# Moving the modulation's vectors one place later in a transformer kernel, and queueing VectorE's part of them behind the MLP step they belong to

## The chip, the cores and the metric

The kernel runs on one core of one Trainium2 chip. The metric is the device time of one execution in microseconds. Work is spread over TensorE (matmuls, with its weight loads beside them), VectorE, ScalarE and GpSimd; all loads of this kernel are issued from SyncE's queue.

## The reference

One token block of 256 tokens with 1024 features goes through two blocks of layers. The first has a mixer (a gated MLP over tokens beside a linear recurrence) and a mixture of 32 experts. The second has two layers, the first with a sparse attention of three branches, the second with a differential attention, and an MLP behind each. In the second block a condition vector modulates every layer:

```
cond = silu(c)                                    # 1024 values
for i in range(2):
    mod = cond @ w_ada[i] + b_ada[i]              # 6 vectors of 1024
    sh1, sc1, g1, sh2, sc2, g2 = split(mod, 6)
    h = rms_norm(x, ln_mix_g[i]) * (1 + sc1) + sh1
    x = x + g1 * mixer_i(h)
    h = rms_norm(x, ln_mlp_g[i]) * (1 + sc2) + sh2
    x = x + g2 * (square(relu(h @ w_mlp_in[i])) @ w_mlp_out[i])
```

The kernel numbers these vectors 0 to 11: vector 6 i + 0 and 1 are shift and scale in front of the mixer of layer i, 2 its gate, 3 and 4 shift and scale in front of the MLP, 5 the MLP's gate. Each is the product of 1024 condition values with a matrix of 1024 x 1024, 4 MB of weights that are read once.

## The kernel before, in words

**Order of work.** The program is written with a framework that plans the order of instructions on each engine and each queue: instructions are written down in program order, and a planner that simulates the engines with its own costs picks, at each point, an instruction whose inputs it takes to be ready, earlier ones first. An instruction may thus run well ahead of the place where it is written. `tc.issue_after(ins)` keeps the instructions that are written inside it behind `ins` on the engine of `ins`. On the chip each engine then works through its planned list.

**Weights.** Every weight tile of 1 MB is loaded by `load` (line 131) from SyncE's queue into one of eight buffers of a ring; a load waits until a buffer has been read out. Matmul operands are split into a high and a low part (`whi` by ScalarE at line 151, `wlo` by VectorE at line 152, in three buffers each), and three products are summed.

**The modulation's vectors.** `ada_at` holds which vector is next and how far it is. There are two ways to make one:

- On TensorE, in two halves. `ada_half` runs `ada_tiles`: two loads of 1 MB and 16 matmuls, each of which uses a strip of 32 columns of the array (line 187; two records each in the trace), then one VectorE copy or addition into `adaacc` (lines 211, 214).
- On VectorE, in four quarters. `ada_vector` loads 1 MB and multiplies it by the condition, one operation for each of its two rows of 1024 (lines 256 and 258), summed in `adasum`. Behind the fourth quarter TensorE sums over the partitions with four strip matmuls against ones, and ScalarE copies the result.

`ada_close` ends a vector: four small products with `pick` (line 225), and a VectorE addition of the bias that writes `mods[v]` (line 228). It is called where the next piece of a vector begins, or where `ada_until` or the second half of an out-projection (`out_late`) asks for it.

Where they stand before: five halves in the first block, seven in the sparse attention (`work(j)` for j = 3 to 9; this makes vectors 2 to 5 complete), vectors 6 to 10 as quarters in the first MLP (`vectors` is 11), and vector 11 in four fills of one tile at the end of that MLP and in the norm behind it (`Stats.fill`). The second MLP is called with `vectors` 12, at which nothing is left.

**The attention.** `attention` runs over 16 units (head pair i, token half m), three stages deep: `pair_probs` of unit j (scores, maximum, exponential), `pair_out` of unit j - 1 (reciprocal, gate, scaling of the probabilities `p`, transposes, product with the values), `pair_tail` of unit j - 2, and `work(j)` in between, which from j = 10 on adds the first half of the out-projection (`oearly`). The second half (`olate`) follows behind the last unit, and feeds the MLP's input through `feed`.

**The MLP.** `mlp` has nine steps. Step j makes 512 hidden features (`hp`, line 448, 96 products), scales, squares and splits them (`relu`, `hid`, lines 1739 to 1745), and then adds the previous step's hidden features to the result (`rows`, line 491, 96 products). From j = 1 on, each step may call `ada_vector` twice behind the hidden features and once between the two halves of `rows`.

Of the kernel before, what the change touches and what calls it, by code (L numbers as in the profile page):

```python
# [13 lines left out]
F32 = mybir.dt.float32  # L14
# [7 lines left out]
ALU = mybir.AluOpType  # L22
# [22 lines left out]
def block_kernel(ctx: ExitStack, tc: tile.TileContext, A: dict, out: bass.AP):  # L45

    nc = tc.nc
# [8 lines left out]
    def mm(shape=(P, 512), name="mm"):  # L56
        return mm_pool.tile(list(shape), F32, tag="mm", name=name)
# [4 lines left out]
    def sc(shape=(P, 512), name="sc"):  # L62
        return scratch.tile(list(shape), F32, tag="sc", name=name)
# [61 lines left out]
    def load(src, c, pool=None, tag="w", cut=1):  # L125

        t = (pool or next(source[0])).tile([P, 2048], F32, tag=tag, name="w")
        v = t[:, : src.shape[1] * c].rearrange("p (k c) -> p k c", c=c)
        n = src.shape[1] // cut
        for i in range(cut):  # L130
            loaded.append(nc.sync.dma_start(v[:, i * n : (i + 1) * n, :], src[:, i * n : (i + 1) * n, :]))
        load_small(SMALL)
        return v
# [40 lines left out]
    mods = [const.tile([P, KD], F32, name=f"mod{v}") for v in range(12)]  # L174
# [9 lines left out]
    def strips(ps, lhsT, w, start, stop):  # L184

        for j in range(4):
            nc.tensor.matmul(ps[32 * j : 32 * j + 32, :], lhsT, w[:, j * T : (j + 1) * T], start=start, stop=stop)  # L187
# [30 lines left out]
    def ada_close():  # L218

        if not ada_open:  # L220
            return
        v = ada_open.pop()
        sp = mm(name="adasum")
        for c in range(2):
            nc.tensor.matmul(
                sp[:, 4 * c : 4 * c + 4], ada_acc[:, c * P : (c + 1) * P], pick, start=True, stop=True
            )
        nc.vector.tensor_tensor(
            mods[v].rearrange("p (j c) -> p c j", c=2),
            sp[:, 0:8].rearrange("p (c j) -> p c j", c=2),  # L230
            col("ada", v * KD, KD).rearrange("p (j c) -> p c j", c=2),
            op=ALU.add,
        )

    def ada_half(behind=(None,)):
        for _ in ada_tiles(behind):
            pass
# [4 lines left out]
            ada_at[2] -= 2.0  # L242
            ada_half()

    def ada_vector(acc):

        ada_close()
        v, q, _ = ada_at
        lay, i = divmod(v, 6)
        w = load(  # L250
            A["w_ada_2"][lay, 2 * q * P : 2 * (q + 1) * P, i * D : (i + 1) * D].rearrange("(k p) c -> p k c", p=P), D
        )
        for kk in range(2):
            c = cond[:, 2 * q + kk : 2 * q + kk + 1]
            if q + kk == 0:
                nc.vector.tensor_scalar(acc, w[:, kk, :], c, None, op0=ALU.mult)
            else:
                nc.vector.scalar_tensor_tensor(acc, w[:, kk, :], c, acc, op0=ALU.mult, op1=ALU.add)
        ada_at[1] = q + 1
        if q == 3:  # L260
            ps = mm(name="adaps")[:, :T]
            strips(ps, ones[:, 0:32], acc, True, True)
            nc.scalar.copy(ada_acc, ps)
            ada_at[:2] = [v + 1, 0]
            ada_open.append(v)
# [247 lines left out]
    def add_pair(pr, bank, gate=None):  # L513

        v = res[:, 2 * pr : 2 * pr + 2, :]
        if gate is None:
            added[0] = nc.vector.tensor_tensor(v, bank, v, op=ALU.add)
        else:
            for j in range(2):
                k = 2 * pr + j  # L520
                nc.vector.scalar_tensor_tensor(
                    res[:, k, :], bank[:, j, :], gate[:, k : k + 1], res[:, k, :], op0=ALU.mult, op1=ALU.add
                )
        return v

    def closing(banks, gate=None, st=None, each=None, feed=None):

        def after(pr):  # L530
            v = add_pair(pr, banks[pr], gate)
            last = pr == KD // 2 - 1
            if feed is not None:
                feed(pr)
                st.square(pr, v)
                if pr >= 2:
                    st.count(pr - 2)
                return
            if st is not None:
                if last and st.w is not None:  # L540
                    held["first"]["dve"] = added[0]
                st.square(pr, v)
            if st is not None:
                for p in range(pr - 2, pr + 1 if last else pr - 1):
                    if last and p == pr and st.w is None:
                        st.fill()
                    if p >= 0:
                        st.count(p)
            if each is not None:
                for p in range(pr - 1, pr + 1 if last else pr):  # L550
                    if p >= 0:
                        each(p)

        return after
# [96 lines left out]
    with tc.tile_pool(name="pa", bufs=1, reuse_waits="tile") as pa:  # L651

        def pt(name, shape=(P, 4, T), tag=None, dt=F32):
            return pa.tile(list(shape), dt, name=name, tag=tag or name)
# [145 lines left out]
        q = pt("q")  # L800
# [200 lines left out]
        r = rstd_of(gss, P, "v")  # L1001
        for m in range(2):
            for h in range(4):
# [5 lines left out]
                    op0=ALU.mult,  # L1009
                    op1=ALU.mult,  # L1010
# [21 lines left out]
        for g in range(4):  # L1032
# [5 lines left out]
                op0=ALU.add,  # L1038
                op1=ALU.mult,
# [37 lines left out]
    with (  # L1077
# [6 lines left out]
        def bt(name, shape, dt=F32, tag=None):  # L1084
# [30 lines left out]
            op=ALU.add,  # L1115
# [23 lines left out]
        for i in range(2):  # L1139
# [5 lines left out]
                op=ALU.is_equal,  # L1145
# [478 lines left out]
        st = Stats(finsq)  # L1624
# [8 lines left out]
    def ct(name, shape, dt=F32, tag=None, **kw):  # L1633
        return pc.tile(list(shape), dt, name=name, tag=tag or name, **kw)

    def n8(name, dt=F32):
        return pc.tile([P, 2048], dt, tag="n8", name=name, bufs=2)
# [80 lines left out]
    def mlp(lay, close, st, vectors):  # L1718

        ada_sum = ct("adasum", (P, D), tag="klo")  # L1720
        if ada_at[1]:
            ada_half()
        w_i, w_o = A["w_mlp_in_2"][lay], A["w_mlp_out_2"][lay]
        pend = None
        for j in range(9):
            rate[0] = 0.0
            if j < 8:
                hp = [(mm if j else acc)((P, TX), name="hp") for _ in range(4)]
                for n, _ in enumerate(proj_X_steps(w_i, j * 512, hp)):
                    if j == 0 and n == 3:  # L1730
                        st.count(2)
                        st.count(3)
                        rb = st.scale()
                both = n8("hid", F32R).rearrange("p (a k t) -> p a k t", a=2, k=4)
                for i in range(2):
                    r = sc((P, 2, T), name="relu")
                    b = pw.tile([P, 4], F32, tag="nm", name="hb")
                    for c in range(2):
                        nc.vector.tensor_copy(b[:, c : c + 1], hp[2 * i + c][:, T : T + 1])
                        nc.vector.tensor_tensor(r[:, c, :], hp[2 * i + c][:, 0:T], rb, op=ALU.mult)  # L1740
                        nc.scalar.activation(r[:, c, :], r[:, c, :], AF.Relu, bias=b[:, c : c + 1])
                    hi = both[:, 0, 2 * i : 2 * i + 2, :]
                    nc.scalar.activation(hi, r, AF.Square)
                    nc.scalar.activation(r, r, AF.Square)
                    nc.vector.tensor_tensor(both[:, 1, 2 * i : 2 * i + 2, :], r, hi.bitcast(F32), op=ALU.subtract)
                for _ in range(2):
                    if j and ada_at[0] < vectors:
                        ada_vector(ada_sum)
            if j == 0:
                banks = [acc((P, 2, T), name="mlp") for _ in range(4)]  # L1750
            if pend is not None:
                jj, bb = pend
                if jj == 7:
                    ada_close()
                    ada_until(6 * lay + 6)
                for c in (0, 2):
                    if c == 2 and ada_at[0] < vectors:
                        ada_vector(ada_sum)
                    after = close(banks) if jj == 7 and c == 2 else None
                    rows(w_o, jj * 4 + c, banks, (bb[:, 0], bb[:, 1]), c, jj == 0 and c == 0, after)  # L1760
            pend = (j, both)
# [16 lines left out]
    both = mm((P, 2, T), name="rbps")  # L1778
# [378 lines left out]
    def work(j):  # L2157
        chains.tick(3)
        if 1 <= j < 5:
            steps(second, 3)  # L2160
        elif j >= 10:
            steps(first, 1)
        if 3 <= j < 10:
            ada_half()

    attention([(i, m) for i in range(8) for m in (1, 0)], pair_probs, pair_out, pair_tail, work)
# [3 lines left out]
    st_x = Stats(plain=True)  # L2170
# [12 lines left out]
    nc.vector.tensor_tensor(nlam, ls[:, 1:2], ls[:, 0:1], op=ALU.subtract)  # L2183
    nc.vector.tensor_scalar(nlam, nlam, -lam_init, None, op0=ALU.add)
    st = Stats()
    mlp(0, lambda banks: closing(banks, mods[5], st), st_x, 11)


    modulated(st, 1, 0, col("lnx", 8, 8))
# [109 lines left out]
    st = Stats(plain=True)  # L2299
# [46 lines left out]
```

## Time and profile before

| | |
|---|---|
| Median of three runs | 1307.72 us (1306.44 to 1311.22) |
| The profiled execution | 1306.74 us, of which the span of the profile is 1305.0 us |
| Granted clock of TensorE, mean | 0.995 |
| TensorE busy | 97% of the span |
| VectorE, ScalarE busy | 50%, 39% |
| Read from HBM | 371.41 MB, 285 GB/s over the span |

Times in the rows are microseconds from the start of the span. A row of the timeline gives start, busy time, engine, line, operation, output and inputs, the number of instructions that were merged, and in brackets how long the engine stood idle before it and what ended that. Engines are PE (TensorE), DVE (VectorE), ACT (ScalarE), POOL (GpSimd), SPq (SyncE's queue of loads). Matmuls overlap in a pipeline, so the sum of their durations is more than the time they take.

### The profile page before, as it was taken

What the parts mean: (1) busy time and instruction counts of PE and PEld (TensorE: products, weight loads), DVE (VectorE), ACT (ScalarE), POOL (GpSimd) and SP (SyncE); (2) the same over time, 40 slices, a digit from 0 to 9 for tenths busy, and PEclk for the clock granted to TensorE, in tenths of its full rate; (3) what the DMA queues carried; (4) which work ended last, traced back from release to release, by engine and by line L of the source; (5) the groups of instructions that cost most, each with busy time, mean ns of one, the idle gap of its engine ahead of it and who ended that gap; (6) DMA issues with size and microseconds to landing.
All of it is one profiled execution on the core that took longest, in us unless ns stands there. A gap on an engine that the chain in (4) does not pass through costs nothing.

```text
span 1305.0 us, 22821 instructions
## 1 busy us (share of the span) xinstructions
PE 1263.6 (97%) x9471; PEld 1001.2 (77%) x9471; DVE 652.6 (50%) x1268; ACT 512.6 (39%) x918; POOL 68.4 (5%) x92
## 2 busy tenths in 40 slices
PE   8999899999999999999999999999999999999998
PEld 7779565665555555556886679999997779999998
DVE  6765310220101111105786777688766777655554
ACT  7743210111101111104555646545444565654644
POOL 1010000000000000000410000000001221000000
PEclk9999999999999999998999999999999999999999
DMA  7997799999999999998545846699677432555510
GB/s 252 369 411 302 305 421 420 420 421 421 422 420 420 421 421 421 420 413 296 186 156 193 323 140 212 206 353 338 244 256 259 161 130 76 180 173 187 194 66 33
DMA packets 99157, 373.98 MB, mean 287 GB/s; under 512 B 10649, under 2 KB 14442, under 8 KB 74730
## 3 DMA queue, kind: packets, MB, share of 16 engines
q1 hardware_dynamic: 99050, 372.49, 74.8%
q8 instruction: 76, 1.25, 0.4%
q14 instruction: 31, 0.25, 0.1%
HBM read 371.41 MB, written 1.05 MB: 285 GB/s over the span
## 4 chain that ended last, share of the span: by engine, by line
PE 74%; issue 11%; DVE 2%; ACT 1%; POOL 0%; DVEq 0%; ACTq 0%; POOLq 0%
PE hp L448 14%; PE mlp L491 14%; PE gups L1413 12%; PE dps L1443 6%; PE dps L469 5%; PE sums L1461 3%; PE gps L1367 2%; PE oearly L584 2%; PE qp L469 2%; PE olate L491 2%; PE adaps L187 1%; PE kv L469 1%; PE opair L2098 1%; PE kcv L469 1%; PE ptps L2089 1%
## 5 line engine op out<-in xcount | busy, mean ns | idle before, releaser
L152 DVE TENSOR_TENSOR wlo<-w,whi 128x1024 fp32r<-128x1024 f32 (+1 forms) x222 | 269.7, 1217 | 158.0 <-ACT whi L151 155.9
L151 ACT CAST whi<-w 128x1024 fp32r<-128x1024 f32 (+1 forms) x222 | 230.4, 1042 | 249.3 <-PE hp L448 105.6
L1413 PE MATMUL gups<-w,xg 128*64 128x256 f32 x2048 | 233.7, 381 | 3.8 <-PEq L1271 2.8
L1413 PEld LDWEIGHTS gups<-w,xg 128*64 128x64 f32 x2048 | 145.1, 137 | 90.0 <-issue 19.4
L491 PE MATMUL mlp<-hid,whi 128*128 128x256 f32 x1024 | 184.0, 282 | 0.0
L491 PEld LDWEIGHTS mlp<-hid,whi 128*128 128x128 f32 x1024 | 157.2, 188 | 0.4 <-issue 0.4
L491 PE MATMUL mlp<-hid,wlo 128*128 128x256 f32 x512 | 144.8, 283 | 0.0
L448 PE MATMUL hp<-hT_lo,whi 128*128 128x258 f32 x512 | 144.0, 282 | 0.0
L448 PE MATMUL hp<-hT_hi,whi 128*128 128x258 f32 x512 | 143.7, 283 | 0.0
L448 PE MATMUL hp<-hT_hi,wlo 128*128 128x258 f32 x512 | 142.5, 282 | 0.0
L1425 DVE TENSOR_TENSOR h<-h,gups 128x256 f32<-128x256 f32 x32 | 13.5, 421 | 235.7 <-ACT h L1424 235.7
L1443 PE MATMUL dps<-w,hT 128*64 128x512 f32 x496 | 112.7, 596 | 5.0 <-ACT hT L1433 5.0
L491 PEld LDWEIGHTS mlp<-hid,wlo 128*128 128x128 f32 x512 | 96.4, 188 | 1.6 <-issue 1.6
L448 PEld LDWEIGHTS hp<-hT_lo,whi 128*128 128x128 f32 x512 | 96.7, 189 | 0.0
L448 PEld LDWEIGHTS hp<-hT_hi,whi 128*128 128x128 f32 x512 | 96.1, 188 | 0.0
L448 PEld LDWEIGHTS hp<-hT_hi,wlo 128*128 128x128 f32 x512 | 95.9, 189 | 0.0
L1424 ACT ACTIVATE h<-gups 128x256 f32<-128x256 f32 x32 | 12.3, 383 | 181.4 <-PE gups L1413 181.4
L1443 PEld LDWEIGHTS dps<-w,hT 128*64 128x64 f32 x496 | 34.1, 137 | 64.3 <-issue 53.0
L1454 DVE COPY ysb<-dps 64x512 f32<-64x512 f32 x31 | 21.2, 683 | 107.1 <-PE dps L1443 107.0
L1455 ACT COPY ysb<-dps 64x512 f32<-64x512 f32 x31 | 18.0, 581 | 139.1 <-DVE ysb L1454 139.1
L1461 PE MATMUL sums<-sw,ysb 128*128 128x256 f32 x256 | 61.3, 385 | 6.3 <-DVE ysb L1454 6.3
L286 POOL TENSOR_TENSOR rs_r<-rs_t,mhalf 128x8 f32<-128x8 f32 (+2 forms) x24 | 36.5, 1521 | 486.4 <-DVE rs_t L280 481.3
(537 smaller groups left out, 2038.4 us busy)
## 6 DMA issues: line engine op xcount, KB each, us to landing
w<-in_w_gate_dram SPq DMA_DIRECT2D x64, 1024.0 KB
w<-in_w_up_dram SPq DMA_DIRECT2D x64, 1024.0 KB
w<-in_w_down_dram SPq DMA_DIRECT2D x62, 1024.0 KB
w<-in_w_ada_dram SPq DMA_DIRECT2D x48, 1024.0 KB
w<-in_w_mlp_in_dram SPq DMA_DIRECT2D x32, 1024.0 KB
w<-in_w_mlp_out_dram SPq DMA_DIRECT2D x32, 1024.0 KB
w<-in_diff_w_in_dram SPq DMA_DIRECT2D x12, 1024.0 KB
w<-in_w_in_dram SPq DMA_DIRECT2D x10, 1024.0 KB
```

The lines of the kernel that those rows point to most:

```text
L151: nc.scalar.copy(hi, v)
L152: nc.vector.tensor_tensor(lo, v, hi.bitcast(F32), op=ALU.subtract)
L286: nc.gpsimd.tensor_tensor(r, t, m, op=ALU.pow)
L448: nc.tensor.matmul(outs[h], a[:, kk, h * P : (h + 1) * P], b[:, k, :], start=(k == 0 and i == 0), stop=(k == KD - 1 and i == 2),)
L469: nc.tensor.matmul(outs[m], b[:, k, m * P : (m + 1) * P], a[:, kk, :], start=(k == 0 and i == 0), stop=(k == KD - 1 and i == 2),)
L491: nc.tensor.matmul(outs[dc // 2][:, dc % 2, :], a[:, 0, dc * P : (dc + 1) * P], b[:, a0 + kk, :], start=(first and kk == 0 and i == 0 and ...
L584: nc.tensor.matmul(banks[h // 2][:, h % 2, :], a[:, kk, h * P : (h + 1) * P], b[:, k, :], start=(k == 0 and i == 0 and h % 2 == 0), stop=( ...
L1367: nc.tensor.matmul(ps[:, j, :], part[:, m, k * P : (k + 1) * P], hot[:, m].rearrange("p e s -> p (e s)"), start=(n == 0), stop=(n == 3),)
L1413: nc.tensor.matmul(ps[j * 64 : (j + 1) * 64, s * 256 : (s + 1) * 256], xg[:, k, s0 : s0 + SLOTS], w[k // 4][:, k % 4, j * 256 : (j + 1) * ...
L1443: nc.tensor.matmul(dps[half * 64 : (half + 1) * 64, :], hT[:, c, j * 64 : (j + 1) * 64], dt[f // 2][:, f % 2, half * 512 : (half + 1) * 51 ...
L1454: nc.vector.tensor_copy(t[e2 * 64 : e2 * 64 + 64, 0:512], dps[0:64, :])
L1461: nc.tensor.matmul(sums[k // 2][:, k % 2, :], t[:, k * P : (k + 1) * P], sw, start=(pr == 0 and k % 2 == 0), stop=(after is not None and k ...
```

## The change

The sparse attention calls `ada_half` for j = 3 to 7 only, so that it makes two halves (one vector) less. The first MLP is called with 10 in place of 11: it makes vectors 5 to 9 as quarters, in place of 6 to 10. The fills at its end make vector 10 in place of 11. Vector 11 is made by the second MLP, which is called with 12 as before and now has one vector left to make. Apart from that, `ada_vector` is given an instruction `behind`: the last VectorE operation on the hidden features of the step in which it is called (`low`). Its VectorE operations are kept behind that one. Its load is not.

```diff
-    def ada_vector(acc):
+    def ada_vector(acc, behind):
...
         for kk in range(2):
             c = cond[:, 2 * q + kk : 2 * q + kk + 1]
-            if q + kk == 0:
-                nc.vector.tensor_scalar(acc, w[:, kk, :], c, None, op0=ALU.mult)
-            else:
-                nc.vector.scalar_tensor_tensor(acc, w[:, kk, :], c, acc, op0=ALU.mult, op1=ALU.add)
+            with tc.issue_after(behind.ins):
+                if q + kk == 0:
+                    nc.vector.tensor_scalar(acc, w[:, kk, :], c, None, op0=ALU.mult)
+                else:
+                    nc.vector.scalar_tensor_tensor(acc, w[:, kk, :], c, acc, op0=ALU.mult, op1=ALU.add)
...
-                    nc.vector.tensor_tensor(both[:, 1, 2 * i : 2 * i + 2, :], r, hi.bitcast(F32), op=ALU.subtract)
+                    low = nc.vector.tensor_tensor(both[:, 1, 2 * i : 2 * i + 2, :], r, hi.bitcast(F32), op=ALU.subtract)
                 for _ in range(2):
                     if j and ada_at[0] < vectors:
-                        ada_vector(ada_sum)
+                        ada_vector(ada_sum, low)
...
                     if c == 2 and ada_at[0] < vectors:
-                        ada_vector(ada_sum)
+                        ada_vector(ada_sum, low)
...
-        if 3 <= j < 10:
+        if 3 <= j < 8:
             ada_half()
...
-    mlp(0, lambda banks: closing(banks, mods[5], st), st_x, 11)
+    mlp(0, lambda banks: closing(banks, mods[5], st), st_x, 10)
```

## Rows read from the trace of the kernel before

**Rows 1.** The page's first part: busy time, share of the span, instructions.

```profile
PE 1263.6 (97%) x9471; PEld 1001.2 (77%) x9471; DVE 652.6 (50%) x1268; ACT 512.6 (39%) x918; POOL 68.4 (5%) x92
```

**Rows 2.** All waits of TensorE from 787 to 990: total, times, longest.

```profile
PE rbps L358 <- POOL rs_r L286: 0.9, 1, 0.9
```

**Rows 3.** Windows: length; busy PE, PEld, DVE, ACT, POOL; clock; DMA share; GB/s.

```profile
720.00:740.00 20.00, 18.33 (x187) 11.72 (x186) 16.54 (x45) 12.70 (x39) 0.00 (x0) 1.00 0.94 348
...
726.80:737.70 10.90, 10.62 (x112) 6.46 (x108) 8.81 (x25) 6.53 (x21) 0.00 (x0) 1.00 0.99 368
...
767.00:774.00 7.00, 7.00 (x65) 6.70 (x64) 7.00 (x15) 0.72 (x2) 0.00 (x0) 1.00 0.73 262
774.00:781.00 7.00, 4.28 (x31) 3.06 (x30) 2.33 (x4) 2.95 (x4) 0.00 (x0) 1.00 0.59 195
...
859.48:883.56 24.08, 24.08 (x206) 23.53 (x206) 21.77 (x30) 12.28 (x18) 0.00 (x0) 1.00 0.98 353
```

**Rows 4.** TensorE's timeline, the attention's last two halves and a close.

```profile
728.55 0.61 PE L225 MATMUL adasum<-pick,adaacc 128*128 128x4 f32 x4
729.44 1.93 PE L187 MATMUL adaps<-w,cond 128*32 128x256 f32 x32 [0.28 <-ACT pt L2091]
...
733.91 1.91 PE L187 MATMUL adaps<-w,cond 128*32 128x256 f32 x26
```

**Rows 5.** VectorE's groups from 762.6 to 774: count, busy us, mean ns.

```profile
L258 DVE SCALAR_TENSOR_TENSOR adasum<-w,cond,adasum 128x1024 f32<-128x1024 f32 x5 | 6.4, 1282 | 0.0
...
L521 DVE SCALAR_TENSOR_TENSOR res<-oearly,mod,res 128x256 f32<-128x256 f32 x4 | 1.7, 473 | 0.0
...
L256 DVE TENSOR_SCALAR adasum<-w,cond 128x1024 f32<-128x1024 f32 x1 | 0.7, 748 | 0.0
```

**Rows 6.** VectorE's timeline, the last unit's softmax.

```profile
767.13 0.17 DVE L2079 RECIPROCAL sm<-sm 128x4 f32<-128x4 f32 x1
...
770.64 0.16 DVE L2080 TENSOR_TENSOR sm<-sm,gate 128x4 f32<-128x4 f32 x1
...
771.91 0.88 DVE L2082 TENSOR_SCALAR p<-p,sm 128x128 f32<-128x128 f32 x4
```

**Rows 7.** TensorE's timeline, the waits at the attention's end.

```profile
775.00 0.66 PE L2098 MATMUL opair<-pt,vv 128*64 128x128 f32 x8 [0.73 <-ACT pt L2091]
...
777.21 0.51 PE L491 MATMUL olate<-oT,whi 128*128 128x256 f32 x2 [0.92 <-DVE oT L566]
...
780.47 0.38 PE L491 MATMUL olate<-oT,wlo 128*128 128x256 f32 x1 [0.76 <-DVE wlo L152]
```

**Rows 8.** TensorE's waits from 980 to 1115, the second out-projection's.

```profile
PE olate L491 <- DVE wlo L152: 0.6, 1, 0.6
```

**Rows 9.** The chain that ended last: starts of successive MLP steps, both layers.

```profile
848.01 11.47 PE hp L448 x96
...
872.09 11.47 PE hp L448 x96
...
1149.97 11.46 PE hp L448 x96
...
1172.83 11.46 PE hp L448 x96
```

**Rows 10.** TensorE's timeline, the attention's first unit.

```profile
686.99 1.19 PE L2089 MATMUL ptps<-ident,p 128*128 128x128 f32 x6 [4.28 <-DVE p L2082]
```

**Rows 11.** Windows behind that gap; columns as in rows 3.

```profile
686.00:688.00 2.00, 1.01 (x7) 0.93 (x8) 1.96 (x9) 1.39 (x8) 1.41 (x1) 0.86 0.00 0
688.00:690.00 2.00, 2.00 (x8) 1.20 (x6) 1.88 (x9) 0.66 (x2) 0.00 (x0) 0.50 0.01 4
690.00:692.00 2.00, 2.00 (x12) 1.19 (x11) 0.79 (x2) 1.51 (x5) 0.00 (x0) 0.79 0.00 0
```

**Rows 12.** SyncE's queue, 790 to 990: one wait, one load's timeline.

```profile
SPq L131 <- DVE adasum L258: 56.0, 15, 5.3
...
846.45 1.50 SPq L131 DMA_DIRECT2D w<-in_w_mlp_in_dram  x2
```

## The prediction

> **What bounds the kernel now.** The page's busy table comes first: TensorE is busy for 1263.6 of 1305.0 us, 97% of the span [rows 1]. A change that moves VectorE's work can therefore only count where TensorE stands still, or where TensorE's own work shrinks. The change touches four places: the end of the first attention (724 to 788 us), the first MLP (788 to 978), the second attention's end (about 1100) and the second MLP (1114 to 1305). For each I ask the list of TensorE's waits and then the timeline.
>
> In the first MLP the list of waits has one entry, 0.9 us behind the POOL reciprocal root at its very end [rows 2]: nothing that VectorE does there holds TensorE up, not even in a step in which VectorE is busy for 21.77 of 24.08 us [rows 3]. In the attention before it the reader is to see two different stretches. From 726.8 to 737.7 TensorE is busy for 10.62 of 10.90 us, and two of the seven halves of a modulation vector lie in there; from 774 to 781 it is busy for only 4.28 of 7.00 [rows 3]. The 7 us before that hole, 767 to 774, have VectorE busy for 7.00 of 7.00, and five accumulations and the product that opens them, all for the first vector of the MLP, are among what it does [rows 3, 5]. They ran ahead of the step that they were written for, because their weights had landed.
>
> **The change, part by part.**
>
> *Two halves leave the attention.* `work(8)` and `work(9)` issue no `ada_half` any more. A half is 32 matmul records in 1.93 us; the second one stands in two pieces, 26 records of it in 1.91 us [rows 4]. With them goes one closing `pick` product out of this stretch (0.61 us): the vector that is closed at 728.55 is now closed behind the attention, where the next vector's close stood until now. The most that can be gained is 2 x 1.93 + 0.61 = 4.5 us. Least is nothing, if the attention's own chain (scores, maximum, exponential, scaling, transposes) sets the pace there and TensorE merely idles where the halves stood. The row between: VectorE is busy for 8.81 of the 10.90 us [rows 3]; three copies or additions of `adaacc` go, 128 x 256 like the residual additions that take 0.47 [rows 5], which leaves about 7.4, so that VectorE would allow the stretch to shrink by 10.90 - 7.4 = 3.5 us. Out-projection work that could fill TensorE is written only from `work(10)` on. I take 3.0, near the VectorE bound, and keep 0 and 4.5 for the range. Four loads of 1 MB leave SP's queue here too; no row has TensorE waiting for a load in this stretch, so I book nothing for them.
>
> *VectorE's operations for the first vector leave the attention's end.* They are 5 x 1.28 + 0.75 = 7.1 us between 762.7 and 774 [rows 5]. VectorE takes its operations in the program's order, and the last unit's softmax is caught among them: its reciprocal is at 767.13, the next tiny operation on it only at 770.64, the scaling of the four blocks at 771.91 [rows 6]; with only the residual additions (1.7 us, [rows 5]) and a split beside it, it could have been at some 768. From the scaling hangs all that TensorE then waits for: `pt` 0.73, `oT` 0.92, and, since the buffers of the weights' splits come free late, `whi` and then `wlo` 0.76 [rows 7]. The hole is 7.00 - 4.28 = 2.7 us [rows 3]. The out-projection of the other layer, which has no such VectorE work in front of it, still shows 0.6 on `wlo` [rows 8]; I take 2.7 - 0.6 = 2.1, and keep 0 and 2.7.
>
> *The first MLP.* It still makes five vectors, 20 quarters of one load and two VectorE operations, now vectors 5 to 9 in place of 6 to 10. Each costs TensorE the summing strips and the pick: a step with one takes 872.09 - 848.01 = 24.08 us, a step of the second MLP without takes 1172.83 - 1149.97 = 22.86 [rows 9], so 1.22 us per vector, five before and five after: nothing. All 40 VectorE operations now start behind the step's own last subtraction. Some eight of them, which ran before the MLP's second step, come to lie behind it. The steps then hold three quarters each, six operations of up to 1.28 us or 7.7 us of VectorE work [rows 5], which is about what the step with 21.77 us of it holds already without a wait of TensorE [rows 2, 3]. Queued behind the gated operations are the splits of the next weights, at most one 1.28 us operation at a time, since the accumulations hang on each other; I book 0.
>
> *What the gate makes late.* The gated tiles hold their ring buffers until then, and SP issues its loads in order; that is a rival below. Vector 4 is closed behind the attention now, vector 10 ahead of the second out-projection. Each is a scale that the following MLP's input needs: pick 0.61, then three tiny VectorE operations at 0.16 to 0.18 [rows 4, 6], some 1.2 us, which the out-projection of 48 and more matmuls hides. Uncovered, it is 1.2 us at each of two places; I book 0.
>
> *One vector more in the second MLP.* Vector 11 is made there from j = 1 on: four loads, eight VectorE operations, strips and pick. The fills at the end of the first MLP stay, with vector 10. TensorE is never idle in those steps, so the 1.22 us count in full [rows 9]. VectorE is far from full there and covers its 9.7 us; uncovered it would still wait only for the next split.
>
> The sum: -3.0 - 2.1 + 1.2 = -3.9 us. The profiled execution took 1306.74 us for its span of 1305.0 and lies 1.0 below the median of 1307.72; the same difference on the median gives 1303.8. By bounds: -4.5 - 2.7 + 1.2 = -6.0 at best, and 0 + 0 + 1.2 + 2.4 = +3.6 at worst without a new stall.
>
> [...]
>
> **The rivals.**
>
> 1. *Nothing to be had.* The attention is paced by VectorE and by its own latency, and TensorE idles where the halves were; only the tail gains. For it speaks VectorE at 7.00 of 7.00 just after; against it TensorE's 10.62 of 10.90 [rows 3]. -2.1 + 1.2 = -0.9, with the tail's gain lost too +1.2: 1306.8 to 1308.9.
> 2. *Both gain in full, and the new order is better as well.* With four loads fewer the out-projection's weights are there earlier, and a new order may close the smaller waits as well, 20.00 - 18.33 = 1.7 us from 720 to 740 [rows 3]. -6.0 - 1.7 = -7.7: 1300.0. Against it: the order is a planner's, and it sees the waits only as its own costs show them.
> [...]
> 4. *The ring starves (slower).* Eight buffers carry all weights. In the first MLP, SP already waited 15 times for an accumulation to free one, 56.0 us in all [rows 12]; now up to three tiles per step sit until the step's last subtraction. Today the weights for a step are asked for 25.6 us ahead (846.45 for the step at 872.09) [rows 9, 12]. It decides from the point at which the gated tiles sit longer than that lead. Then each step waits for about one load: 1.05 MB at the 353 GB/s of a step with the DMA 0.98 busy [rows 3] is 3.0 us, and seven steps make 21: 1307.7 - 3.9 + 21 = 1325. Against it: the gate opens once per 24 us step, and a step needs seven loads, 21 us at that rate.
>
> **How the numbers follow.** What a measurement of this kernel can tell from no change is about 0.5%, 6.5 us: below 1301.2 it is faster, above 1314.3 slower. The forecast (-2 to -6 us) has a chance of 0.55, rival 1 0.19, rival 2 0.13, rival 3 0.05, rival 4 0.08. Faster is rival 2 and the lower edge of the forecast, with runs that scatter by some us: 0.13 + 0.05 = 0.18. Slower is rival 4 and a little of the rest: 0.09. Same is what is left, 0.73. The range takes in the forecast and rivals 1 and 3, leaves out rival 4 and the lower half of rival 2: 1299.5 to 1309.0.
>
> **What would show it.** The profile after should have 12 halves on TensorE in place of 14 and 48 strip records in place of 40; the first accumulation of `adasum` behind the second step's last subtraction and none before the MLP; the last unit's scaling right behind its reciprocal, and the waits on `pt` and `oT` at the end of the attention gone; the first MLP's steps unchanged at 22.9 to 24.1 us; one step of the second MLP at 24.1. The prediction is wrong if waits for `whi` or for loads appear in the first MLP, if TensorE's idle time between 726 and 740 grows by about what was removed, or if a wait for a modulation vector stands in front of either MLP.

## The result and the profile after

The changed kernel takes 1325.36 us (median of four runs, 1324.32 to 1326.41) against 1308.55 (1306.44 to 1311.22) for the kernel before: a ratio of 1.0129, with a 95% interval of 1.0111 to 1.0147. It is 16.8 us slower, and lies far outside the range that was forecast. The profiled execution has a span of 1322.6 us, against 1305.0 before.

The page's first part shows little of it: TensorE's share of the span fell by one point [rows 1].

```profile
PE 1269.3 (96%) x9415; PEld 1007.3 (76%) x9415; DVE 661.2 (50%) x1274; ACT 513.0 (39%) x919; POOL 67.5 (5%) x92
```

Cut by stages, the 17.6 us between the two profiled spans are found at once. The stages are cut at the same work in both traces: the second step's first product in the first MLP (823.93 before, 819.80 after), the backbone product behind that MLP (988.21 and 1002.94), the second MLP's first full product (1125.65 and 1141.98), and the end. The first cut is even only to 0.25 us: by the two timelines that product starts at 823.77 and at 819.89. Counted from those two starts, the kernel gains 3.9 us up to the first cut. The first MLP loses 18.6, the second attention 1.6, the second MLP 1.3; together 17.6, the whole difference.

The losing stage in one window each; first the kernel before:

```profile
823.93:988.21 164.28, 163.31 (x1398) 156.99 (x1396) 124.69 (x173) 82.96 (x115) 1.62 (x1) 0.99 0.79 282
```

and after:

```profile
819.80:1002.94 183.14, 170.39 (x1400) 163.10 (x1398) 131.54 (x177) 82.77 (x115) 1.62 (x1) 0.94 0.78 275
```

The columns are those of rows 3. TensorE does the same work, 1398 and 1400 records. Its idle time goes from 164.28 - 163.31 = 1.0 us to 183.14 - 170.39 = 12.8, and the work takes 7.1 us more of busy time (6.8 counted from the same product), at a mean clock of 0.94 in place of 0.99. So nearly two thirds of the loss are waiting, 11.8 us, and the rest is a lower clock. The list of TensorE's waits for that stage (total, times, longest), which before had the one entry of [rows 2], names the waits:

```profile
PE adaps L187 <- DVE adasum L260: 9.8, 2, 6.2
PE adasum L225 <- ACT adaacc L265: 1.9, 3, 0.7
PE ssps L330 <- DVE sq L320: 1.0, 1, 1.0
```

TensorE waits for the last accumulation of a vector, because the strips that sum it over the partitions stand in its list. TensorE's timeline shows where they stand:

```profile
842.84 0.64 PE L187 MATMUL adaps<-adasum,ones 128*32 128x256 f32 x8
844.19 0.61 PE L225 MATMUL adasum<-pick,adaacc 128*128 128x4 f32 x4 [0.72 <-ACT adaacc L265]
...
871.40 0.64 PE L187 MATMUL adaps<-adasum,ones 128*32 128x256 f32 x8 [3.57 <-DVE adasum L260]
872.52 1.01 PE L225 MATMUL adasum<-pick,adaacc 128*128 128x4 f32 x4 [0.48 <-ACT adaacc L265]
...
905.29 1.08 PE L187 MATMUL adaps<-adasum,ones 128*32 128x256 f32 x8 [6.21 <-DVE adasum L260]
906.30 0.58 PE L450 MATMUL hp<-hT_hi,whi 128*128 128x258 f32 x1
...
985.84 0.64 PE L187 MATMUL adaps<-adasum,ones 128*32 128x256 f32 x8
```

Behind each of the first three rows with strips begin the next step's `hp` products. They need nothing of the vector; they are queued behind it, as the row at 906.30 shows. VectorE's timeline ahead of the longest wait:

```profile
892.90 1.29 DVE L1747 TENSOR_TENSOR hid<-relu,hid 128x512 fp32r<-128x512 f32 x2
894.10 1.28 DVE L260 SCALAR_TENSOR_TENSOR adasum<-w,cond,adasum 128x1024 f32<-128x1024 f32 x1
895.30 1.22 DVE L152 TENSOR_TENSOR wlo<-w,whi 128x1024 fp32r<-128x1024 f32 x1
896.43 1.28 DVE L260 SCALAR_TENSOR_TENSOR adasum<-w,cond,adasum 128x1024 f32<-128x1024 f32 x1
897.63 1.22 DVE L152 TENSOR_TENSOR wlo<-w,whi 128x1024 fp32r<-128x1024 f32 x1
898.77 1.28 DVE L260 SCALAR_TENSOR_TENSOR adasum<-w,cond,adasum 128x1024 f32<-128x1024 f32 x1
900.08 1.23 DVE L152 TENSOR_TENSOR wlo<-w,whi 128x1024 fp32r<-128x1024 f32 x1
901.22 3.92 DVE L260 SCALAR_TENSOR_TENSOR adasum<-w,cond,adasum 128x1024 f32<-128x1024 f32 x3
```

The step's last subtraction (L1747) ends at 894.2, and six accumulations follow, three of them with a split of a weight between. The last ends at 905.1. TensorE finished the step's 192 products at about 899.1 and stands still for 6.21 us. The waits follow the number of accumulations that a vector still needs behind the gate. With three quarters a step and four a vector that is 2, 4, 6, 2 and 4 for the five vectors in turn: no wait at 842.84, 3.57 us at 871.40, 6.21 us at 905.29, and again none for the fourth, at 954.3. The fifth needs 4 and makes no wait either. Its last accumulation ends at 982.7, and its strips stand at 985.84 among the MLP's last products in `rows`, not ahead of another step. The number of accumulations thus counts only together with the place of the strips in TensorE's list.

Behind the two waits comes most of the rest of the loss, in windows of 2 us (the clock is the third column from the right):

```profile
872.00:874.00 2.00, 1.52 (x10) 1.48 (x8) 1.87 (x2) 0.37 (x1) 0.00 (x0) 0.59 1.07 376
874.00:876.00 2.00, 2.00 (x11) 2.00 (x11) 0.25 (x2) 0.00 (x0) 0.00 (x0) 0.50 0.89 303
876.00:878.00 2.00, 2.00 (x11) 2.00 (x11) 0.00 (x0) 0.00 (x0) 0.00 (x0) 0.50 1.04 357
878.00:880.00 2.00, 2.00 (x15) 2.00 (x14) 0.00 (x0) 0.52 (x1) 0.00 (x0) 0.71 0.91 355
...
906.00:908.00 2.00, 2.00 (x12) 1.70 (x9) 0.00 (x0) 0.37 (x1) 0.00 (x0) 0.50 1.05 339
908.00:910.00 2.00, 2.00 (x11) 2.00 (x11) 0.00 (x0) 0.00 (x0) 0.00 (x0) 0.53 0.93 343
```

The granted clock is 0.50 to 0.71 from 872 to 880 us, behind the first wait, and 0.50 and 0.53 from 906 to 910, behind the second; from 880 to 882 and from 910 to 912 it is 1.00. The chain that ended last gives the price, three steps' 96 `hp` products [rows 9]:

```profile
873.54 14.16 PE hp L450 x96
...
906.37 13.27 PE hp L450 x96
...
931.47 11.47 PE hp L450 x96
```

14.16 - 11.47 = 2.7 and 13.27 - 11.47 = 1.8 us for the same 96 products. Ahead of them the four `pick` products at 872.52 took 1.01 us, at 844.19 0.61, and the eight strip records at 905.29 took 1.08 us, at 842.84 0.64; by windows of 4 us, some 5.5 us of the clock's loss lie behind the two waits. Some 1.6 us more lie at the MLP's end, where the clock is at 0.93, 0.50 and 0.64 in three windows from 991.8 to 1002.94, and in the kernel before at 0.57 in one, 983.93 to 987.93.

### The profile page after: what moved, and what is told of

Read it like the earlier page. It is cut to its first block, busy times and chain, and to the rows that moved or that the text cites. A ratio compares the mean times of both kernels' runs of the same rounds, so it can differ in the third digit from the quotient of the medians.

```text
span 1322.6 us, 22703 instructions
## 1 busy us (share of the span) xinstructions
PE 1269.3 (96%) x9415; PEld 1007.3 (76%) x9415; DVE 661.2 (50%) x1274; ACT 513.0 (39%) x919; POOL 67.5 (5%) x92
## 5 line engine op out<-in xcount | busy, mean ns | idle before, releaser
L1457 ACT COPY ysb<-dps 64x512 f32<-64x512 f32 x31 | 18.0, 582 | 139.0 <-DVE ysb L1456 139.0
L1463 PEld LDWEIGHTS sums<-sw,ysb 128*128 128x128 f32 x256 | 46.4, 190 | 20.0 <-DVE ysb L1456 13.3
```

The source lines that it names most:

```text
L1457: nc.scalar.copy(t[e2 * 64 : e2 * 64 + 64, 512:1024], dps[64:128, :])
L1463: nc.tensor.matmul(sums[k // 2][:, k % 2, :], t[:, k * P : (k + 1) * P], sw, start=(pr == 0 and k % 2 == 0), stop=(after is not None and k ...
```

## The experiments

The main theory was that the gate delays the last accumulation of a vector and the strips hand the delay to TensorE. The rivals were that the moved vectors do the harm, that VectorE's work is too much behind the second step, or that a bank of PSUM held by the strips keeps the next products back. The kernel before was timed beside each set: median 1308.75 us (25 runs) with the first four kernels, 1307.17 us (23 runs) with the last four.

**The gate alone.** The change without its shift:

```diff
-        if 3 <= j < 8:
+        if 3 <= j < 10:
...
-    mlp(0, lambda banks: closing(banks, mods[5], st), st_x, 10)
+    mlp(0, lambda banks: closing(banks, mods[5], st), st_x, 11)
```

> The gate without the move: vectors stay where they were (seven halves in the attention, 6 to 10 in the first MLP), only VectorE's operations for them are kept behind the last subtraction of their own step. Theory A (the gate makes the last accumulation of a vector late, and the summing strips stand in TensorE's list ahead of the next step's products, so that the list stands still) expects the same waits on the accumulation as in the changed kernel, 9 to 11 us in two steps, and the lower clock behind them: 1322 to 1327 us. Theory B (the moved vectors do the harm: another vector in the second MLP, another set of loads) expects no such wait and about 1306.

It takes 1327.64 us (two runs), ratio 1.0147 (1.0122 to 1.0172), a little above the range expected by theory A. The three entries of its waits in the first MLP are those of the changed kernel to the tenth, of which the first:

```profile
PE adaps L187 <- DVE adasum L260: 9.8, 2, 6.2
```

The gate alone brings the whole loss.

**The shift alone.** The reverse of the diff above, on the kernel before: two halves less in the first attention and vector 11 in the second MLP, but no gate.

> The move without the gate. Theory A expects no wait of TensorE on an accumulation in the first MLP, some 2.5 us less in the attention, 1.2 us more in the second MLP: 1306 to 1308 us. Theory B expects most of the loss of the changed kernel, 1320 or more.

1313.12 us, ratio 1.0036 (1.0024 to 1.0049). No wait for an accumulation in the first MLP, as expected; the time is what neither theory expected. The second attention takes 144.38 us (986.78 to 1131.16) in place of 137.44. Six of the eight operations for vector 11, written for the second MLP's later steps, ran ahead into that attention, as six did in the first one before [rows 5]. VectorE's timeline shows two of them in a softmax:

```profile
1073.50 0.75 DVE L256 TENSOR_SCALAR adasum<-w,cond 128x1024 f32<-128x1024 f32 x1
1074.17 0.61 DVE L1703 TENSOR_REDUCE dnm<-scores 128x1 f32<-128x256 f32 x2
1074.70 0.16 DVE L2227 RECIPROCAL dsm<-dsm 128x2 f32<-128x2 f32 x1
1074.78 1.26 DVE L258 SCALAR_TENSOR_TENSOR adasum<-w,cond,adasum 128x1024 f32<-128x1024 f32 x1
```

TensorE's waits in that stretch have one of 3.1 us, where the kernel before has one of 1.2, and the clock is low behind it:

```profile
PE ptps L1711 <- DVE dss L2268: 3.1, 1, 3.1
```

The windows there, with the clock as above:

```profile
1076.00:1080.00 4.00, 2.30 (x7) 1.67 (x7) 3.20 (x12) 0.48 (x1) 1.01 (x1) 0.53 0.70 225
1080.00:1084.00 4.00, 4.00 (x16) 3.28 (x16) 3.32 (x7) 1.85 (x8) 0.00 (x0) 0.50 0.09 37
```

The mean clock of the stage is 0.96, before 1.00. So the gate is worth something where it was not looked for: it keeps vector 11 out of the second attention, which takes 139.04 us in the changed kernel.

**The strips later.** The whole change, with two accumulators in turn, and the strips issued only in the step after the one that ends the vector:

```diff
+        acc = acc[:, v % 2, :]
...
         if q == 3:
+            ada_due.append((v, acc))
+            ada_at[:2] = [v + 1, 0]
...
+    def ada_total():
+        if ada_due:
+            v, acc = ada_due.pop()
...
-        ada_sum = ct("adasum", (P, D), tag="klo")
+        ada_sum = ct("adasum", (P, 2, D), tag="klo")
...
+                ada_total()
                 for _ in range(2):
                     if j and ada_at[0] < vectors:
...
                 if jj == 7:
+                    ada_total()
```

> The changed kernel, gate and move kept, but the summing strips of a vector are written one step later, behind the next step's hidden features, and two accumulators are used in turn so that the next vector doesn't wait for the strips. Theory A expects the waits on the accumulation to vanish though VectorE's operations are as late as before: 1304 to 1307 us. Theory C (VectorE is too full once all forty operations lie behind the second step, wherever the strips stand) expects the wait to come back in another form, on the split of the weights or on a later strip: 1315 or more.

1308.85 us, ratio 1.0000 (0.9990 to 1.0009). The same gate and the same load on VectorE, and the waits for accumulations are gone. Of the list only this is left in the first MLP:

```profile
PE ssps L338 <- DVE sq L328: 1.0, 1, 1.0
```

This is the cleanest test of the cause: nothing on VectorE was relieved, save that a new vector need not wait for the strips of the last. It lies above its expected range. The stage takes 165.82 us, 1.5 more than before, at the same idle time of 1.0 us; what it loses is clock, at 0.89 from 960 to 990. The last vector's strips stand there among the MLP's last products, as in the changed kernel, but that they are the reason is not shown.

**The gate one step earlier.** The accumulations of a step behind the last subtraction of the step before:

```diff
+                gate_at = low if j else None
...
-                        ada_vector(ada_sum, low)
+                        ada_vector(ada_sum, gate_at)
```

> The changed kernel with the operations of a step kept behind the last subtraction of the step before it, so that they have a whole step more. Theory A expects no wait on an accumulation, and the tail of the attention as free as in the changed kernel: 1304 to 1307 us. Theory C expects VectorE still too full from the first step on: 1312 or more.

1305.44 us, ratio 0.9975 (0.9964 to 0.9985): the one kernel here that beats the kernel before, by 3.3 us, which is under the 0.5% that was set as the bound. The accumulations run during the step's `hp` products, and TensorE's strips find them done. The first MLP takes 162.69 us, 1.6 less than before, but that is not the gate's work: it takes 162.64 in the kernel with the shift alone, and what the kernel before has more is the window at a clock of 0.57 at its end.

**The gate at the first step only.** All accumulations of an MLP behind the subtraction of its step 0:

```diff
+                first_low = first_low if j else low
...
-                        ada_vector(ada_sum, low)
+                        ada_vector(ada_sum, first_low)
```

> The changed kernel, with every accumulation of an MLP queued behind the first step's last subtraction, and no later one. The theory of the late last accumulation expects no wait for an accumulation in the first MLP and 1304 to 1307 us, like the gate one step earlier. The rival, that it is the amount of VectorE's work in the later steps that is too much (40 operations in seven steps), expects the same waits as in the changed kernel and 1320 us or more, since the amount is the same.

1307.04 us, ratio 0.9996 (0.9986 to 1.0006), with no wait for an accumulation. All 40 operations still lie behind step 0, so the amount isn't what hurts. This kernel has the same shift as the one before it and, like it, no wait for an accumulation, and yet no gain that can be told from nothing.

**Four quarters a step.** The opposite: each vector ends in the step that begins it, so that eight accumulations stand between the gate and the strips.

```diff
-                for _ in range(2):
+                for _ in range(3):
```

> The changed kernel with four quarters of a vector in each step in place of three: each vector is finished in the step that began it, so eight accumulations stand between the gate and the strips in each of five steps, and the last two steps have none. VectorE's total is the same. The theory of the late last accumulation expects a wait of 8 to 10 us in front of the strips in five steps, each with the lower clock behind it: 1350 to 1375 us. The rival of the total amount expects no more than the changed kernel's 1325 us.

1365.91 us in one run. TensorE's waits, the first of the list:

```profile
PE adaps L187 <- DVE adasum L260: 53.1, 6, 8.9
```

Five of the six waits are in the first MLP, one in the second. Behind each, the `hp` products took 12.5 to 13.9 us in place of 11.47. With 2, 4, 6 and 8 accumulations behind the gate, the longest wait is thus 0, 3.57, 6.21 and 8.9 us: from four on, two more accumulations cost about 2.7, two operations of 1.28 us [rows 5].

**Two banks of PSUM.** The changed kernel with the four accumulators of `hp` in two banks, two fewer. The product is made over 256 of its 258 columns, and so the kernel leaves out the true bias of the hidden features:

```diff
-                                b[:, k, :],
...
+                                b[:, k, 0:T],
...
-                hp = [(mm if j else acc)((P, TX), name="hp") for _ in range(4)]
+                two = [(mm if j else acc)((P, 2, T), name="hp") for _ in range(2)]
+                hp = [two[h // 2][:, h % 2, :] for h in range(4)]
```

> The changed kernel, with the MLP input product's four accumulators in two PSUM banks in place of four, so that the modulation's two products never share the last free banks with them. It leaves out the 258th column of that product (the bias), so its time is that of the schedule alone. The theory that the gate makes the last accumulation late expects the same three waits for it, 9 to 11 us together, and about 1322 us. The rival, that a bank of PSUM that the strips hold keeps the next step's products back, expects no wait for an accumulation and about 1303 us.

1326.48 us in one run, and the same wait:

```profile
PE adaps L187 <- DVE adasum L260: 9.8, 2, 6.2
```

A shortage of PSUM banks is thus not what makes the wait.

**The gate one step earlier, no shift.** The gate of the 1305.44 us kernel with the diff of the first experiment.

> The kernel before, with the accumulations of an MLP step queued behind the subtraction of the step before it, and no vector moved. If the gain of the gate one step earlier with the shift (ratio 0.9975) comes from the shift, this one takes the time of the kernel before, 1308 to 1309 us; if the gate alone frees the attention's tail (-1 to -2 us), 1306 to 1308 us. No wait for an accumulation in either case.

1306.48 us, ratio 0.9995 (0.9985 to 1.0004). The two cases that were set apart lie too close for the runs to choose between them by the ratio. By its waits the gate does free the attention's tail: before, they were 0.73 on `pt`, 0.92 on `oT`, 0.31 on `whi` and 0.76 on `wlo`; here `pt` is gone and `oT` is 0.3, 1.3 us less. What the shift adds on top of a harmless gate is not shown. By the ratios of the two sets, 0.9975 against 0.9995, it would be a gain of about 2.6 us; in the set of this run, the gate at the first step has the shift and takes 1307.04 us, 0.6 more than this kernel.

## Why the prediction was wrong

*The first MLP.* The stage was booked at 0 and lost 18.6 us, 11.8 of waiting and 6.8 of clock. Here it failed, where VectorE's 7.7 us per step were found harmless because they are "about what the step with 21.77 us of it holds already without a wait of TensorE", and the whole was closed with "I book 0". That step holds no wait because its accumulations are spread over it and no result of them was due at its end: the strips of the kernel before stand about 20 products into `rows` (861.78 in the step whose `rows` begin at 859.48, [rows 3]), behind accumulations of which the last had started at 855.91 and was done 4.6 us earlier:

```profile
855.91 1.28 DVE L258 SCALAR_TENSOR_TENSOR adasum<-w,cond,adasum 128x1024 f32<-128x1024 f32 x1
...
861.78 0.64 PE L187 MATMUL adaps<-adasum,ones 128*32 128x256 f32 x8
```

The gate moves the end of a chain against its deadline, and not an amount. The prediction named what is queued behind the gated operations on VectorE (the splits), and didn't follow the gated result to the engine that consumes it. On TensorE the strips stand ahead of 96 products that need nothing of them and start behind them all the same (906.30). The opening sentence had the same gap: it let a move of VectorE's work count only where TensorE stood still already, and not where it makes a new wait. The later strips, the earlier gate and the four quarters each moved this one distance, and the waits went to none, to none and to 53.1 us.

The prediction's own test was also too narrow: it would have called itself wrong at waits for `whi` or loads, and the wait that came was for `adasum`.

*The starving ring* was the rival that gave 1325, almost the measured time, by a mechanism that did not happen; that the two numbers agree is chance. SyncE's queue waited for accumulations 57.2 us in 17 waits from 790 to 1003, before 56.0 in 15 [rows 12]; with the strips later, 54.8 in 19 and the time of the kernel before. No wait of TensorE in the first MLP is for a load.

*The clock* stands in no term of the sum of -3.9. Rival 3, with its chance of 0.05, was a lower clock in the attention at a price of 1.7 us, what the windows of [rows 11] lose behind the gap of [rows 10]: 0.28 + 1.00 + 0.42. No run shows that price for the places the halves left: from 720 to 740 the clock is 1.00 before [rows 3] and after (below). In the first MLP, where nothing was put for it, the clock cost some 7 us: behind the 3.57 and 6.21 us waits it was 0.50.

*The attention's halves and its tail* were put at -3.0 - 2.1 = -5.1; to the first cut the profiled gain is 3.9. Two windows of the trace after:

```profile
720.00:740.00 20.00, 16.86 (x156) 11.71 (x148) 15.15 (x48) 11.04 (x41) 0.00 (x0) 1.00 0.63 220
760.00:780.00 20.00, 18.93 (x157) 17.02 (x157) 10.80 (x25) 9.27 (x22) 0.00 (x0) 1.00 0.25 86
```

The tail's hole of 2.7 us [rows 3] is 20.00 - 18.93 = 1.07 now: the waits on `pt` and `oT` of [rows 7] are gone, 0.3 on `whi` and 0.8 on `wlo` remain. So its term was about 1.65, where 2.1 was put. That leaves some 2.3 for the halves, where 3.0 was put. Of the 4.5 us of TensorE work that left, 1.5 came back as waits: from 720 to 740 TensorE idles for 3.14 us, before 1.67 [rows 3]. Another 0.4 had been lost ahead of the change's first place, where the first unit's transposes start at 687.41 and before at 686.99 [rows 10].

Two readings behind these terms were wrong. The bound from VectorE took three operations on `adaacc` out of the stretch; the one at 728.08 belongs to a half that stays, so that two of 0.42 us go and the bound is about 3.0 and not 3.5. And only three of the six operations of [rows 5] lie in the 7 us before the hole; the others start at 762.70, 763.96 and 765.93. The step named for the tail is confirmed, the scaling now stands right behind its reciprocal [rows 6]:

```profile
763.51 0.17 DVE L2081 RECIPROCAL sm<-sm 128x4 f32<-128x4 f32 x1
763.71 0.17 DVE L2082 TENSOR_TENSOR sm<-sm,gate 128x4 f32<-128x4 f32 x1
763.91 0.88 DVE L2084 TENSOR_SCALAR p<-p,sm 128x128 f32<-128x128 f32 x4
```

*One vector more in the second MLP* was put at +1.22 and measured +1.3.

*The second attention* was booked at 0 and lost 1.6 us, all of it clock: the one wait of 1.2 us is in both traces, and the clock from 1080 to 1100 is 0.91 after and 1.00 before. The stage takes 139.0 us as well in the last kernel of the experiments (985.95 to 1124.96), whose second attention is that of the kernel before, so the change is not shown to be the reason.

With the gate one step earlier the kernel gains 3.3 us, interval -4.7 to -2.0, which is near the sum of -3.9; with the gate at the first step, which makes nothing late either, the ratio is 0.9996. How far the whole sum holds is thus left open. What sank the forecast is the term that was booked at nothing.

## What to carry to other kernels

When operations are held back on one engine, find the last result of the held chain, the instruction on another engine that takes it, and what stands behind that instruction in its list: the cost is decided there, by the time between gate and deadline, and not by how busy the held engine is. Here VectorE at 21.77 of 24.08 us made no wait of TensorE [rows 2, 3], and six accumulations between gate and strips made one of 6.21 us. A busy share that was harmless before says nothing once the work has a deadline. A gate can be right and stand in the wrong place: the same gate one step earlier kept its use and cost nothing (1305.44 us, and 1308.75 for the kernel before).

## What was not expected of the hardware

The same gap is not always granted the same clock. In the two stretches below, TensorE's busy time in the changed kernel and in that with the gate one step earlier is the same to 0.01 us, and the longest gap ahead of the second, 4.3 us, is the same too. The clock is 0.91 and 0.93 in the one and 0.87 and 0.78 in the other. From the changed kernel:

```profile
600.00:640.00 40.00, 36.94 (x173) 30.19 (x173) 29.95 (x54) 22.16 (x36) 13.11 (x19) 0.91 0.62 199
690.00:700.00 10.00, 10.00 (x87) 6.17 (x85) 5.63 (x19) 5.85 (x21) 0.00 (x0) 0.93 0.15 39
```

and from the kernel with the gate one step earlier:

```profile
600.00:640.00 40.00, 36.94 (x170) 30.38 (x167) 30.02 (x54) 21.94 (x36) 11.13 (x18) 0.87 0.61 190
690.00:700.00 10.00, 10.00 (x77) 6.99 (x79) 6.02 (x20) 5.56 (x21) 0.00 (x0) 0.78 0.01 2
```

40 x 0.04 + 10 x 0.15 = 3.1 us would be lost in the second trace by these means, but its windows don't hold the same work, since it is late in them. By the starts of the same products it is between 1.3 and 2.7 us: they come 1.4 us later at 607 us (607.24 and 608.61), 2.1 later behind the gap of 4.3 us (687.41 and 689.50), where six of them take 1.12 and 1.51 us, and 2.7 later at the second step of the first MLP (819.9 and 822.6). The 1.2 us wait in the second attention likewise left the clock at 1.00 from 1060 to 1100 in the kernel before; over 20 us from 1080 it was 0.91 in the changed kernel and 0.92 with the strips later, and from 1060 0.92 with the gate one step earlier. What decides it stays open; two profiled executions differ by 1.3 us or more for this alone, where the best version gains 3.3, so that this gain rests on the medians of 12 and 25 runs, not on the profiles.
